# Making the weight sums of a seven-product pair ahead of the ordinary pair before it, in a two-layer hybrid block on Trainium2

## The chip, the core and the metric

The kernel runs on one core of a Trainium2 chip (trn2). The engines that matter are TensorE (PE: matmuls, with its weight loads as PEld), VectorE (DVE), ScalarE (ACT), and SyncE (SP), which issues the loads of the weights. Each engine works through its own list of instructions in the order of that list. The metric is the time of one launch in microseconds (us); lower is better.

## What is computed

Two layers on 256 tokens of width 2048, in float32: a first layer with a state-space branch and sparse attention, and a second one with compressed and selected attention and a gated delta rule. The change touches only large matrix products: one half of the first layer's output projection, both layers' feed-forward parts, two of the second layer's merge products, and its output projection. Cut to these, the reference is:

```python
x = x + concat([y_ssd, y_att]) @ w_out          # 2048 x 2048
u = rmsnorm(x, g_mlp) @ w_up                    # 2048 x 8192
x = x + square(relu(u)) @ w_down                # 8192 x 2048
...                                             # second layer: projections, attention, delta rule
x = x + (g_a * (o_a @ w_pa) + g_b * (o_b @ w_pb)) @ w_o      # g_a, g_b = sigmoid(h @ columns of w_in)
h = rms_norm(x, ln2_w)
out = rms_norm(x + square(relu(h @ w_up)) @ w_down, ln_f_w)
```

## The kernel before

Every weight is read from memory once. Weights and activations are float32 values that the kernel splits into a high and a low part, so a product of one activation block by one weight block is three matmuls: high by high, high by the weights' low part, low by high (`product`, lines 273 to 276). For a weight tile, ScalarE makes the high part (`whi`, line 281) and VectorE the low part by subtracting (`wlo`, line 282). Pools of four tiles each hold `whi` and `wlo`, so the two engines can be at most four tiles ahead of TensorE.

The function `wide` (line 251) multiplies 2048 rows of a weight by 1024 of its columns, in eight **pairs** numbered 0 to 7. A pair is two blocks of 128 rows: one transfer of 1024 KB into a tile `wst` (line 289). Three such tiles exist (`stp`, bufs=3), so the transfer of a pair can only start when the pair three places earlier has been read for the last time. A pair is one of two kinds:

- An **ordinary pair** takes eight products, 24 matmuls of 512 columns. Its weights become two `whi` and two `wlo` tiles of 1024 columns each.
- A **seven-product pair** (a step of the Strassen-Winograd scheme on 2 x 2 blocks) takes seven products, 21 matmuls. For that VectorE first makes sums of its four weight blocks: `t13` with one instruction over 1024 columns (line 303), then the two halves of `t24`, 512 columns each (lines 306 and 307). The `whi` and `wlo` tiles of the pair come in the order: two blocks of the weights themselves, `t13`, `t24`, and a last half tile of the weights.

In text below, a **four-pair call** is a call of `wide` whose pairs 1, 3, 5 and 7 are of the seven-product kind; there are twelve, six in each feed-forward part (three of `w_up`, three of `w_down`). A **three-pair call** has pairs 3, 5 and 7 of that kind; there are sixteen in the feed-forward parts beside the first call of each of them. With two first calls and five calls in the projections that makes 35 calls and 117 seven-product pairs.

Between the calls the results leave the accumulation banks, and each `w_down` call but the last ones adds its result into memory: four transfers of 512 KB each that add to what is there (line 476), issued by GpSimd. They run while the next call has begun.

The kernel's text gives each engine's instructions in program order, and when the program is built, the framework orders every engine's list anew from priorities in that order and its own idea of durations. It also adds all waits. So the list of VectorE is not the order of the text.

Of the kernel before, what the change touches and what calls it, by code (L numbers as in the profile page):

```python
# [13 lines left out]
OP = mybir.AluOpType  # L14
# [43 lines left out]
def build(ctx, tc, I, out, tap=None, upto=99):  # L58
    nc = tc.nc
    V, S, G, PE = nc.vector, nc.scalar, nc.gpsimd, nc.tensor  # L60
# [14 lines left out]
    def sp(shape, dt=F32, name="sp"):  # L75
        return sb.tile(shape, dt, name=name, tag="sp", bufs=NP)
# [13 lines left out]
    def psum(kind, shape):  # L90
        return pp.tile(shape, F32, name=kind, bufs=2)
# [159 lines left out]
    def wide(w, r0, c0, lhs, forms, order=range(8), spairs=None, hooks={}):  # L251


        ka, kb = (("mm0", "mm1"), ("tp", "sx"))[::1 - 2 * (turn[0] % 2)]
        turn[0] += 1
        B = {}

        def banks(tags, *names):
            for k, pair_ in zip(tags, names):
                for b in pair_:  # L260
                    B[b] = psum(k, [128, 512])
        banks(ka, ("P2", "P3"), ("P4", "E"))
        spairs = tuple(forms) if spairs is None else spairs
        ns = len(spairs)
        left = {b: 3 * ns + (0 if b in ("P1", "P5", "P6", "P7") else 6 * (8 - ns)) for b in ("P1", "P2", "P3", "P4", "P5", "P6", "P7", "E")}
        left["E"] = 6 * (8 - ns)
        total = dict(left)

        def mm(b, x, y):
            PE.matmul(B[b], x, y, start=left[b] == total[b], stop=left[b] == 1)  # L270
            left[b] -= 1

        def product(b, xh, xl, wa, wb):
            mm(b, xh, wa)
            mm(b, xh, wb)
            mm(b, xl, wa)

        def parts(src, n=1024):
            a = whp.tile([128, 1024], F32R, name="whi")
            b = wlp.tile([128, 1024], F32R, name="wlo")  # L280
            S.activation(a[:, :n], src, AF.Copy)  # L281
            V.tensor_tensor(b[:, :n], src, a[:, :n].bitcast(F32), op=OP.subtract)  # L282
            return [(a[:, o:o + 512], b[:, o:o + 512]) for o in range(0, n, 512)]

        for j in order:
            if j in hooks:
                hooks[j](kb)
            s = stp.tile([128, 2048], F32, name="wst")
            nc.sync.dma_start(s.rearrange("p (k n) -> p k n", k=2),
                              w[r0 + j * 256:r0 + j * 256 + 256, c0:c0 + 1024].rearrange("(k p) n -> p k n", p=128))  # L290
            if j not in spairs:
                for kk in range(2):
                    xh, xl = lhs(2 * j + kk)
                    wl = parts(s[:, kk * 1024:(kk + 1) * 1024])[::-1]
                    for i, l, b in ((0, 0, "P2"), (0, 1, "P3"), (1, 0, "P4"), (1, 1, "E")):
                        h = slice(i * 128, i * 128 + 128)
                        product(b, xh[:, h], xl[:, h], *wl[l])
                continue
            if "P1" not in B:
                banks(kb, ("P1", "P5"), ("P6", "P7"))  # L300

            t13 = sp([128, 2, 512], name="t13")
            V.tensor_tensor(t13, s.rearrange("p (k l n) -> p k l n", k=2, l=2)[:, :, 0],  # L303
                            s[:, :1024].rearrange("p (l n) -> p l n", l=2)[:, ::-1], op=OP.subtract)
            t24 = sp([128, 2, 512], name="t24")
            V.tensor_tensor(t24[:, 0], s[:, 1024:1536], t13[:, 0], op=OP.subtract)  # L306
            V.tensor_tensor(t24[:, 1], s[:, 1536:], t24[:, 0], op=OP.subtract)  # L307
            (a1h, a1l), (a2h, a2l) = lhs(2 * j), lhs(2 * j + 1)
            m1, m2 = slice(0, 128), slice(128, 256)
            sh, sl = forms[j]  # L310

            def sums(n):
                return sh[:, n - 1], sl[:, n - 1]
            w11, w22 = parts(s[:, 512:1536])
            product("P1", a1h[:, m1], a1l[:, m1], *w11)
            product("P3", *sums(4), *w22)
            u1, u3 = parts(flat(t13))
            product("P5", *sums(1), *u1)
            product("P7", *sums(3), *u3)
            u2, u4 = parts(flat(t24))  # L320
            product("P6", *sums(2), *u2)
            product("P4", a2h[:, m2], a2l[:, m2], *u4)
            (w21,) = parts(s[:, 1536:], 512)
            product("P2", a2h[:, m1], a2l[:, m1], *w21)
        return B, ka
# [67 lines left out]
    def flat(ap):  # L393
        return ap.rearrange("p k c -> p (k c)")
# [14 lines left out]
    def ffn(act, forms, xd, w_up, w_down, late, after, tail=0):  # L409
# [6 lines left out]
        for s_ in range(4):  # L416
            hT, hforms = [], {}
            for P in range(2):
                B, tags = wide(w_up, 0, s_ * 2048 + P * 1024, at_k(act), forms,
                               spairs=NPAIRS[1:] if r is None or P == 1 else NPAIRS,  # L420
                               hooks={2: hook} if r is None else {})
                us = {}
                for i, l, part, bank in shared(B, part_pairs()):
                    V.tensor_tensor(part, bank, part, op=OP.add)
                    S.activation(part, part, AF.Relu, scale=r[:, i:i + 1])
                    S.activation(part, part, AF.Square)
                    us[i, l] = part
                for l in (1, 0):
                    q = quarter("hT")
                    p = len(hT)  # L430
                    hT.append(q)
                    for k0 in range(0, 4, 2):
                        pt = psum(tags[k0 // 2], [128, 512])
                        pv = pt.rearrange("p (k t c) -> p k t c", k=2, t=2)
                        for kk in range(2):
                            for t in range(2):
                                c = (k0 + kk) * 128
                                PE.transpose(pv[:, kk, t, :], us[t, l][:, c:c + 128], ident)
                        j = 2 * p + k0 // 2
                        if j in NPAIRS:  # L440
                            f = two_forms(sp)
                            S.activation(f[0].rearrange("p k t c -> p (k t c)"), pt, AF.Copy)
                            f_to_act(f, q, k0, hforms, j)
                        else:
                            split(pt, flat(q[0][:, k0:k0 + 2]), flat(q[1][:, k0:k0 + 2]))
            for P in range(2):
# [4 lines left out]
                if (s_, P) == (3, 1):  # L451
                    for p in (2, 3):
                        ps = panel(w_down, s_ * 2048, 16, p * 512, 512, at_k(hT), tail=tail if p == 3 else 0)
                        for t in range(2):
                            V.tensor_tensor(X[p][:, t], ps[t], X[p][:, t], op=OP.add)
                            after(p, t)
                    continue
                B, _ = wide(w_down, s_ * 2048, P * 1024, at_k(hT), hforms, spairs=NPAIRS[1 - P:])
                if s_ == 3:
                    add_blocks(B, P, part_pairs())  # L460
# [396 lines left out]
    for p in range(2):  # L857
        ps = panel(I["w_out"][0], 0, 16, p * 512, 512, at_k(mix), order=list(range(8, 16)) + list(range(8)))
        for t in range(2):
            V.tensor_tensor(X[p][:, t], ps[t], X[p][:, t], op=OP.add)  # L860
        x_done(p, xn, g_mlp, ssx, xforms)
    add_blocks(wide(I["w_out"][0], 0, 1024, at_k(mix), forms_of(mix, (6, 0, 2)), (4, 5, 6, 7, 0, 1, 2, 3))[0], 1)

    def late1(tags):
# [605 lines left out]
```

## Time and profile before

| | us |
|---|---|
| median of three runs (lowest, highest) | 2688.77 (2684.59, 2689.42) |
| the profiled execution, its own time | 2686.3 |
| its span in the profile | 2684.5 |
| TensorE busy | 2612.6 (97%) |
| VectorE busy | 2138.8 (80%) |
| ScalarE busy | 1555.9 (58%) |
| granted TensorE clock, mean share of full speed | 0.996 |

The ends of matmuls in the profile are modelled and overlap, so TensorE's busy share says little on how near it is to its best pace; the starts of matmuls do. In the rows, `t` stands for `t13` and `t24`, since numbers are left out, `SPq` is SyncE's queue, and a tile's name before `<-` is what is written.

### The profile page before, as it was taken

The page shows a single profiled execution, that of the slowest core. Times are in us where ns is not written, and L with a number is a line of the kernel's source. Part 1 is how long each engine was busy: PE and PEld are TensorE (multiplying, and loading weights), DVE is VectorE, ACT ScalarE, POOL GpSimd, SP SyncE. Part 2 cuts the span into 40 slices and gives each one's busy share as a digit, 9 for nine tenths or more (in the row PEclk, how much of TensorE's full clock was granted, in tenths as well). Part 3 has the DMA queues.
Part 4 walks back from the last instruction along what each step waited for, and adds up shares of the span by engine and source line. Part 5 has one row for each costly group of instructions (what it writes and reads, how often), then busy time and mean ns, then how long its engine had stood idle before and what let it go on. Part 6 is the DMA issues. An engine that isn't in the chain of part 4 may idle for free.

```text
span 2684.5 us, 33032 instructions
## 1 busy us (share of the span) xinstructions
PE 2612.6 (97%) x12485; PEld 2153.5 (80%) x12485; DVE 2138.8 (80%) x2978; ACT 1555.9 (58%) x2098; POOL 82.6 (3%) x94
## 2 busy tenths in 40 slices
PE   8999999999999999999999999999999999999997
PEld 8988888777777777788888877888777778787776
DVE  5767789888989888676755867588999889898885
ACT  5555556666657566554533654455666566575663
POOL 0000000010000000000000000000000100000000
PEclk9999999999999999999999999999999999999999
DMA  7454555585675776653432843556655866756764
GB/s 234 152 161 162 181 194 204 188 240 199 205 235 188 220 219 204 210 193 126 137 92 81 288 136 125 175 196 214 216 204 188 231 200 205 242 188 220 219 219 141
DMA packets 191133, 512.22 MB, mean 191 GB/s; under 512 B 10151, under 2 KB 51070, under 8 KB 190974
## 3 DMA queue, kind: packets, MB, share of 16 engines
q1 hardware_dynamic: 175600, 467.57, 51.8%
q0 software_dynamic: 6912, 25.17, 5.3%
q10 hardware_dynamic: 8462, 17.37, 1.9%
q8 instruction: 98, 1.61, 0.2%
q14 instruction: 61, 0.50, 0.0%
HBM read 476.51 MB, written 33.57 MB: 190 GB/s over the span
## 4 chain that ended last, share of the span: by engine, by line
PE 63%; DVE 20%; DMA 9%; ACT 5%; issue 3%; ACTq 0%; POOL 0%; POOLq 0%; DVEq 0%; SPq 0%
PE mm L270 12%; PE mm L194 10%; PE mm L193 10%; PE mm L192 10%; DVE wlo L282 10%; PE tp L270 6%; PE sx L270 6%; DMA wst<-in_w_down_dram 4%; DMA wst<-in_w_up_dram 4%; ACT whi L281 3%; DVE t L303 2%; DVE hTl L172 1%; DVE t L307 1%; DVE t L306 1%; DVE sfl L172 1%
## 5 line engine op out<-in xcount | busy, mean ns | idle before, releaser
L282 DVE TENSOR_TENSOR wlo<-wst,whi 128x1024 fp32r<-128x1024 f32 (+1 forms) x560 | 609.2, 1109 | 83.3 <-ACT whi L281 81.5
L281 ACT ACTIVATE whi<-wst 128x1024 fp32r<-128x1024 f32 (+1 forms) x560 | 535.3, 969 | 230.1 <-PE mm L270 70.7
L208 DVE TENSOR_TENSOR wlo<-wst,whi 128x1024 fp32r<-128x1024 f32 (+6 forms) x336 | 377.2, 1128 | 209.2 <-ACT whi L207 208.3
L207 ACT ACTIVATE whi<-wst 128x1024 fp32r<-128x1024 f32 (+6 forms) x336 | 329.3, 983 | 319.6 <-PE mm L194 292.7
L281 ACT ACTIVATE whi<-t 128x1024 fp32r<-128x1024 f32 x234 | 247.7, 1059 | 322.0 <-DVE t L307 206.0
L282 DVE TENSOR_TENSOR wlo<-t,whi 128x1024 fp32r<-128x1024 f32 x234 | 284.4, 1222 | 48.0 <-ACT whi L281 44.6
L194 PE MATMUL mm<-whi,x2l 128*128 128x512 f32 (+3 forms) x608 | 229.4, 377 | 0.0
L193 PE MATMUL mm<-wlo,x2h 128*128 128x512 f32 (+3 forms) x608 | 228.1, 375 | 0.9 <-DVE wlo L208 0.8
L192 PE MATMUL mm<-whi,x2h 128*128 128x512 f32 (+3 forms) x608 | 228.0, 376 | 0.0
L303 DVE TENSOR_TENSOR t<-wst 128x1024 f32<-128x1024 f32 x117 | 142.8, 1221 | 52.5 <-DMA wst<-in_w_down_dram 27.6
L192 PE MATMUL mm<-whi,xnh 128*128 128x512 f32 (+3 forms) x416 | 152.6, 368 | 2.0 <-ACT whi L207 1.6
L193 PE MATMUL mm<-wlo,xnh 128*128 128x512 f32 (+3 forms) x416 | 151.7, 365 | 0.0
L194 PE MATMUL mm<-whi,xnl 128*128 128x512 f32 (+3 forms) x416 | 150.6, 365 | 0.1
L270 PE MATMUL mm<-wlo,xnh 128*128 128x512 f32 x377 | 148.2, 393 | 2.4 <-DVE wlo L282 2.4
L270 PE MATMUL mm<-whi,xnl 128*128 128x512 f32 x377 | 147.4, 391 | 0.0
L270 PE MATMUL mm<-whi,xnh 128*128 128x512 f32 x377 | 143.4, 393 | 0.5 <-DVE ca L336 0.5
L270 PE MATMUL mm<-wlo,hTh 128*128 128x512 f32 x328 | 129.3, 394 | 2.5 <-DVE wlo L282 2.4
L193 PEld LDWEIGHTS mm<-wlo,x2h 128*128 128x128 f32 x608 | 114.5, 188 | 16.8 <-DVE wlo L208 1.6
L270 PE MATMUL mm<-whi,hTl 128*128 128x512 f32 x328 | 127.9, 390 | 0.0
L194 PEld LDWEIGHTS mm<-whi,x2l 128*128 128x128 f32 x608 | 114.5, 188 | 15.3 <-issue 1.0
L270 PE MATMUL mm<-whi,hTh 128*128 128x512 f32 x328 | 126.2, 394 | 0.5 <-DVE ca L336 0.5
L192 PEld LDWEIGHTS mm<-whi,x2h 128*128 128x128 f32 x608 | 114.6, 189 | 15.0 <-issue 0.8
(620 smaller groups left out, 5759.4 us busy)
## 6 DMA issues: line engine op xcount, KB each, us to landing
wst<-in_w_up_dram SPq DMA_DIRECT2D x128, 1024.0 KB, 5.1
wst<-in_w_down_dram SPq DMA_DIRECT2D x128, 1024.0 KB, 5.5
wst<-in_w_in_dram SPq DMA_DIRECT2D x84, 1024.0 KB, 5.0
wst<-in_w_out_dram SPq DMA_DIRECT2D x16, 1024.0 KB, 5.8
wst<-in_w_o_dram SPq DMA_DIRECT2D x16, 1024.0 KB, 5.2
wst<-in_w_in_dram SPq DMA_DIRECT2D x16, 780.0 KB, 4.5
xd<-cd POOLq DMA_DIRECT2D x24, 512.0 KB, 10.1
wst<-in_w_in_dram SPq DMA_DIRECT2D x12, 824.0 KB, 4.6
```

Source lines behind the costliest of these rows:

```text
L172: V.tensor_tensor(lo, ps, hi.bitcast(F32), op=OP.subtract)
L192: PE.matmul(ps[t][:, :n], xh[:, sl], wa, start=kt == first, stop=False)
L193: PE.matmul(ps[t][:, :n], xh[:, sl], wb, start=False, stop=False)
L194: PE.matmul(ps[t][:, :n], xl[:, sl], wa, start=False, stop=kt == last)
L207: S.activation(a[:, :2 * n], src, AF.Copy)
L208: V.tensor_tensor(b[:, :2 * n], src, a[:, :2 * n].bitcast(F32), op=OP.subtract)
L270: PE.matmul(B[b], x, y, start=left[b] == total[b], stop=left[b] == 1)
L281: S.activation(a[:, :n], src, AF.Copy)
L282: V.tensor_tensor(b[:, :n], src, a[:, :n].bitcast(F32), op=OP.subtract)
L303: V.tensor_tensor(t13, s.rearrange("p (k l n) -> p k l n", k=2, l=2)[:, :, 0], s[:, :1024].rearrange("p (l n) -> p l n", l=2)[:, ::-1], op ...
L306: V.tensor_tensor(t24[:, 0], s[:, 1024:1536], t13[:, 0], op=OP.subtract)
L307: V.tensor_tensor(t24[:, 1], s[:, 1536:], t24[:, 0], op=OP.subtract)
```

## The change

For an ordinary pair that a seven-product pair follows, the loop now issues the transfer of the following pair and makes that pair's `t13` and `t24` before it turns to the ordinary pair's own `whi` and `wlo`. The sums are kept until the loop comes to their pair. No instruction is added or taken away. The new helper functions `load` and `sums_of` hold the lines that stood in the loop.

```diff
@@ -282,12 +282,32 @@
             V.tensor_tensor(b[:, :n], src, a[:, :n].bitcast(F32), op=OP.subtract)
             return [(a[:, o:o + 512], b[:, o:o + 512]) for o in range(0, n, 512)]
 
-        for j in order:
-            if j in hooks:
-                hooks[j](kb)
+        def load(j):
             s = stp.tile([128, 2048], F32, name="wst")
             nc.sync.dma_start(s.rearrange("p (k n) -> p k n", k=2),
                               w[r0 + j * 256:r0 + j * 256 + 256, c0:c0 + 1024].rearrange("(k p) n -> p k n", p=128))
+            return s
+
+        def sums_of(s):
+
+            t13 = sp([128, 2, 512], name="t13")
+            V.tensor_tensor(t13, s.rearrange("p (k l n) -> p k l n", k=2, l=2)[:, :, 0],
+                            s[:, :1024].rearrange("p (l n) -> p l n", l=2)[:, ::-1], op=OP.subtract)
+            t24 = sp([128, 2, 512], name="t24")
+            V.tensor_tensor(t24[:, 0], s[:, 1024:1536], t13[:, 0], op=OP.subtract)
+            V.tensor_tensor(t24[:, 1], s[:, 1536:], t24[:, 0], op=OP.subtract)
+            return t13, t24
+
+        order = list(order)
+        ready = {}
+        for n_, j in enumerate(order):
+            if j in hooks:
+                hooks[j](kb)
+            s, ts_ = ready.pop(j, (None, None))
+            s = load(j) if s is None else s
+            if j not in spairs and n_ + 1 < len(order) and order[n_ + 1] in spairs:
+                s_next = load(order[n_ + 1])
+                ready[order[n_ + 1]] = s_next, sums_of(s_next)
             if j not in spairs:
                 for kk in range(2):
                     xh, xl = lhs(2 * j + kk)
@@ -298,13 +318,7 @@
                 continue
             if "P1" not in B:
                 banks(kb, ("P1", "P5"), ("P6", "P7"))
-
-            t13 = sp([128, 2, 512], name="t13")
-            V.tensor_tensor(t13, s.rearrange("p (k l n) -> p k l n", k=2, l=2)[:, :, 0],
-                            s[:, :1024].rearrange("p (l n) -> p l n", l=2)[:, ::-1], op=OP.subtract)
-            t24 = sp([128, 2, 512], name="t24")
-            V.tensor_tensor(t24[:, 0], s[:, 1024:1536], t13[:, 0], op=OP.subtract)
-            V.tensor_tensor(t24[:, 1], s[:, 1536:], t24[:, 0], op=OP.subtract)
+            t13, t24 = sums_of(s) if ts_ is None else ts_
             (a1h, a1l), (a2h, a2l) = lhs(2 * j), lhs(2 * j + 1)
             m1, m2 = slice(0, 128), slice(128, 256)
             sh, sl = forms[j]
```

SyncE's list and GpSimd's have the same instructions in the same order as before. VectorE's list, in a four-pair call (the second half's `w_down`, `wst_7878` is pair 4 and ordinary, the seven-product pair 5 is `wst_7912` before and `wst_7880` now), from the last tile of pair 3 on. Before:

```order
L282 TENSOR_TENSOR wlo_7872<-wst_7834,whi_7871 128x512
L282 TENSOR_TENSOR wlo_7881<-wst_7878,whi_7880 128x1024
L282 TENSOR_TENSOR wlo_7897<-wst_7878,whi_7896 128x1024
L303 TENSOR_TENSOR t13_7914<-wst_7912 128x1024
L282 TENSOR_TENSOR wlo_7920<-wst_7912,whi_7919 128x1024
L306 TENSOR_TENSOR t24_7916<-wst_7912,t13_7914 128x512
L282 TENSOR_TENSOR wlo_7930<-t13_7914,whi_7929 128x1024
L307 TENSOR_TENSOR t24_7916<-wst_7912,t24_7916 128x512
L282 TENSOR_TENSOR wlo_7940<-t24_7916,whi_7939 128x1024
L282 TENSOR_TENSOR wlo_7950<-wst_7912,whi_7949 128x512
L303 TENSOR_TENSOR t13_7992<-wst_7990 128x1024
```

Now:

```order
L282 TENSOR_TENSOR wlo_7872<-wst_7802,whi_7871 128x512
L294 TENSOR_TENSOR t13_7882<-wst_7880 128x1024
L282 TENSOR_TENSOR wlo_7888<-wst_7878,whi_7887 128x1024
L297 TENSOR_TENSOR t24_7884<-wst_7880,t13_7882 128x512
L282 TENSOR_TENSOR wlo_7904<-wst_7878,whi_7903 128x1024
L298 TENSOR_TENSOR t24_7884<-wst_7880,t24_7884 128x512
L282 TENSOR_TENSOR wlo_7920<-wst_7880,whi_7919 128x1024
L282 TENSOR_TENSOR wlo_7930<-t13_7882,whi_7929 128x1024
L282 TENSOR_TENSOR wlo_7940<-t24_7884,whi_7939 128x1024
L282 TENSOR_TENSOR wlo_7950<-wst_7880,whi_7949 128x512
```

The `t13` of pair 5 stood behind both `wlo` tiles of pair 4; now it stands ahead of both, and the two halves of `t24` stand ahead of and behind the second one. Pair 3 is moved in the same way. At pair 7 `t13` stood ahead of pair 6 already, and only the halves of `t24` moved; pair 1 stays as it was.

VectorE's list in a three-pair call (`wst_7541` is the ordinary pair 4), from the last tile of pair 3 on. Before:

```order
L282 TENSOR_TENSOR wlo_7535<-wst_7493,whi_7534 128x512
L282 TENSOR_TENSOR wlo_7544<-wst_7541,whi_7543 128x1024
L282 TENSOR_TENSOR wlo_7560<-wst_7541,whi_7559 128x1024
L306 TENSOR_TENSOR t24_7579<-wst_7575,t13_7577 128x512
L282 TENSOR_TENSOR wlo_7583<-wst_7575,whi_7582 128x1024
L307 TENSOR_TENSOR t24_7579<-wst_7575,t24_7579 128x512
L282 TENSOR_TENSOR wlo_7593<-t13_7577,whi_7592 128x1024
L282 TENSOR_TENSOR wlo_7603<-t24_7579,whi_7602 128x1024
L282 TENSOR_TENSOR wlo_7613<-wst_7575,whi_7612 128x512
L303 TENSOR_TENSOR t13_7655<-wst_7653 128x1024
L282 TENSOR_TENSOR wlo_7622<-wst_7619,whi_7621 128x1024
```

Now:

```order
L282 TENSOR_TENSOR wlo_7535<-wst_7461,whi_7534 128x512
L297 TENSOR_TENSOR t24_7547<-wst_7543,t13_7545 128x512
L282 TENSOR_TENSOR wlo_7551<-wst_7541,whi_7550 128x1024
L298 TENSOR_TENSOR t24_7547<-wst_7543,t24_7547 128x512
L282 TENSOR_TENSOR wlo_7567<-wst_7541,whi_7566 128x1024
L282 TENSOR_TENSOR wlo_7583<-wst_7543,whi_7582 128x1024
L282 TENSOR_TENSOR wlo_7593<-t13_7545,whi_7592 128x1024
L282 TENSOR_TENSOR wlo_7603<-t24_7547,whi_7602 128x1024
L282 TENSOR_TENSOR wlo_7613<-wst_7543,whi_7612 128x512
L294 TENSOR_TENSOR t13_7623<-wst_7621 128x1024
L282 TENSOR_TENSOR wlo_7629<-wst_7619,whi_7628 128x1024
```

The two `t24` instructions of pair 5 moved ahead of the two `wlo` tiles of pair 4; the `t13` of pair 7 stood ahead of the tiles of pair 6 in both.

TensorE's list at the start of pair 2 (`hTh` and `hTl` are the activations) of the same four-pair call. Before:

```order
L270 MATMUL mm0_7714<-whi_7802,hTh_6980 128x512
L270 MATMUL mm0_7714<-wlo_7803,hTh_6980 128x512
L270 MATMUL mm0_7714<-whi_7802,hTl_6981 128x512
L270 MATMUL mm0_7715<-whi_7802,hTh_6980 128x512
L270 MATMUL mm0_7715<-wlo_7803,hTh_6980 128x512
L270 MATMUL mm0_7715<-whi_7802,hTl_6981 128x512
```

Now:

```order
L270 MATMUL mm0_7714<-whi_7809,hTh_6980 128x512
L270 MATMUL mm0_7715<-whi_7809,hTh_6980 128x512
L270 MATMUL mm1_7716<-whi_7809,hTh_6980 128x512
L270 MATMUL mm1_7717<-whi_7809,hTh_6980 128x512
L270 MATMUL mm0_7714<-wlo_7810,hTh_6980 128x512
L270 MATMUL mm0_7714<-whi_7809,hTl_6981 128x512
```

Four matmuls that need only `whi` now come ahead of the first that needs `wlo`. At pair 4 and pair 6 of a four-pair call TensorE's list is as before: the second matmul needs `wlo`.

## Rows read from the trace of the kernel before

**Rows 1.** The page, part 1: busy time of each engine, share of the span, instructions.

```profile
PE 2612.6 (97%) x12485; PEld 2153.5 (80%) x12485; DVE 2138.8 (80%) x2978; ACT 1555.9 (58%) x2098; POOL 82.6 (3%) x94
```

**Rows 2.** Groups by line: busy us, mean ns of one, idle before, its releasers.

```profile
L282 DVE TENSOR_TENSOR wlo<-wst,whi 128x1024 fp32r<-128x1024 f32 (+1 forms) x560 | 609.2, 1109 | 83.3 <-ACT whi L281 81.5
...
L303 DVE TENSOR_TENSOR t<-wst 128x1024 f32<-128x1024 f32 x117 | 142.8, 1221 | 52.5 <-DMA wst<-in_w_down_dram 27.6 <-DMA wst<-in_w_up_dram 23.3 <-DMA wst<-in_w_in_dram 0.8
...
L307 DVE TENSOR_TENSOR t<-wst,t 128x512 f32<-128x512 f32 x117 | 80.2, 685 | 0.1
```

**Rows 3.** Waits over the whole span: total us, times, longest us.

```profile
ACT whi L281 <- DVE t L307: 206.0, 88, 3.8
```

**Rows 4.** Timeline, VectorE, one call: start, us, line, out<-in, count [idle before <-releaser].

```profile
906.21 2.96 DVE L282 TENSOR_TENSOR wlo<-wst,whi 128x512 fp32r<-128x512 f32 x3
...
916.14 3.15 DVE L282 TENSOR_TENSOR wlo<-wst,whi 128x512 fp32r<-128x512 f32 x3
921.59 1.23 DVE L303 TENSOR_TENSOR t<-wst 128x1024 f32<-128x1024 f32 x1 [2.31 <-DMA wst<-in_w_down_dram]
...
930.38 2.35 DVE L282 TENSOR_TENSOR wlo<-wst,whi 128x1024 fp32r<-128x1024 f32 x2
```

**Rows 5.** Timeline, TensorE, the same call.

```profile
918.74 0.39 PE L270 MATMUL mm<-whi,hTh 128*128 128x512 f32 x1
918.97 0.39 PE L270 MATMUL mm<-wlo,hTh 128*128 128x512 f32 x1
...
927.52 0.50 PE L270 MATMUL sx<-whi,sfh 128*128 128x512 f32 x1 [0.36 <-ACT whi L281]
928.78 0.50 PE L270 MATMUL sx<-wlo,sfh 128*128 128x512 f32 x1 [0.76 <-DVE wlo L282]
...
931.65 0.50 PE L270 MATMUL mm<-wlo,hTh 128*128 128x512 f32 x1 [0.54 <-DVE wlo L282]
```

**Rows 6.** Timeline, SyncE, the same call: the loads of pairs 5 and 7 issued.

```profile
909.20 0.37 SPq L289 DMA_DIRECT2D wst<-in_w_down_dram  x1
...
919.31 0.37 SPq L289 DMA_DIRECT2D wst<-in_w_down_dram  x1
```

**Rows 7.** The page, part 6: a load, KB each, median us from issue to landing.

```profile
wst<-in_w_down_dram SPq DMA_DIRECT2D x128, 1024.0 KB, 5.5
```

**Rows 8.** Window, same call: us, busy by engine, granted clock, DMA share, GB/s.

```profile
913.00:921.00 8.00, 8.00 (x37) 6.61 (x36) 4.97 (x6) 3.72 (x4) 0.00 (x0) 1.00 1.03 274
```

**Rows 9.** Timeline, VectorE: the same wait in the first and the twelfth such call.

```profile
564.31 1.23 DVE L303 TENSOR_TENSOR t<-wst 128x1024 f32<-128x1024 f32 x1 [2.19 <-DMA wst<-in_w_down_dram]
...
2509.78 1.23 DVE L303 TENSOR_TENSOR t<-wst 128x1024 f32<-128x1024 f32 x1 [2.73 <-DMA wst<-in_w_up_dram]
```

**Rows 10.** Timeline, VectorE, a call with three seven-product pairs.

```profile
874.63 2.96 DVE L282 TENSOR_TENSOR wlo<-wst,whi 128x512 fp32r<-128x512 f32 x3
...
885.29 1.23 DVE L303 TENSOR_TENSOR t<-wst 128x1024 f32<-128x1024 f32 x1 [2.33 <-DMA wst<-in_w_down_dram]
886.44 2.36 DVE L282 TENSOR_TENSOR wlo<-wst,whi 128x1024 fp32r<-128x1024 f32 x2
```

**Rows 11.** Timeline, TensorE and then SyncE, that call.

```profile
887.71 0.50 PE L270 MATMUL tp<-wlo,hTh 128*128 128x512 f32 x1 [1.28 <-DVE wlo L282]
...
877.62 0.37 SPq L289 DMA_DIRECT2D wst<-in_w_down_dram  x1
```

**Rows 12.** Windows at three long TensorE waits, columns as in group 8.

```profile
1048.80:1056.00 7.20, 4.92 (x22) 3.81 (x21) 7.20 (x9) 4.56 (x5) 0.00 (x0) 1.00 0.09 14
1077.00:1081.00 4.00, 0.07 (x2) 0.03 (x1) 4.00 (x8) 1.00 (x3) 0.00 (x0) 1.00 0.69 266
1081.70:1085.10 3.40, 2.93 (x10) 2.65 (x11) 3.40 (x6) 1.96 (x5) 0.00 (x0) 0.50 0.55 219
2593.80:2596.40 2.60, 0.08 (x1) 0.00 (x0) 2.60 (x5) 1.05 (x2) 0.00 (x0) 1.00 0.23 80
2597.20:2600.60 3.40, 3.40 (x9) 2.64 (x9) 3.40 (x5) 1.14 (x2) 0.00 (x0) 0.50 0.22 48
```

## The prediction

> **What bounds the kernel now.** I read the busy times first, then the groups by line and the waits, and then one call of `wide` as a timeline. TensorE is busy 2612.6 us of the span [rows 1]. Its matmuls of 512 columns start 0.23 us apart [rows 5], so only the places where the starts are further apart can be won or lost. The change moves work on VectorE, so I ask where TensorE waits for VectorE in a call, and what VectorE waited for in turn.
>
> A four-pair call shows it. VectorE finishes the `wlo` tiles of pair 4 at 919.29 (916.14 + 3.15), then is idle for 2.31 us until the transfer of pair 5 lands, and makes its `t13` from 921.59 on [rows 4]. TensorE had begun pair 4 at 918.74 with a product of `whi`, and its first `wlo` product at 918.97 did not wait [rows 5]. It waits only later: 927.52, 928.78 (both in pair 5) and 931.65 (the first `wlo` of pair 6) are starts after a wait [rows 5]. Between 918.97 and 931.65 lie 24 + 21 = 45 matmuls, which need 10.20 us at 0.2267 us; they took 12.68. So this call loses 2.48 us there. All twelve four-pair calls have this wait of VectorE for the transfer of pair 5; the first and the last of them are in [rows 9].
>
> The transfer is late because it shares the DMA engines: from 913 to 921 they are fully busy (share 1.03, 274 GB/s) [rows 8], with the adds into memory of the call before. It was issued at 909.20, the moment that VectorE had read pair 2 for the last time (906.21 + 2.96 = 909.17) [rows 4, 6], since three `wst` tiles rotate. So the issue of a load hangs on VectorE's list, and not on where the load stands in the program.
>
> **The change part by part.** Nothing is added or removed: 117 `t13` of 1.22 us and 234 halves of `t24` of 0.685 us [rows 2] are made in either kernel.
>
> *The loads.* SyncE's list is unchanged and its loads are gated by the three tiles, so "one pair ahead" moves no issue forward. It moves some back: the last reading of pair 2 now stands behind `t13` and half of `t24` of pair 3. Successive VectorE instructions overlap by some 0.08 us, so that is about 1.14 + 0.60 = 1.74 us later. Whether the landing moves is the unknown. The DMA engines are busy anyway with the load of pair 4 and the adds [rows 8], and the load of pair 5 would stand in line behind pair 4's; so between 0 and 1.74 us. I take 0.25, near the lower end, because the window shows no free engine that an earlier issue could have used.
>
> *Pair 4 in a four-pair call (the main term).* The `wlo` tiles of pair 4 now stand behind `t13` of pair 5, which cannot start before the landing at 921.59. VectorE keeps its order, so the first `wlo` of pair 4 ends at 921.59 + 1.14 + 1.22 = 923.95 and TensorE can take it at 924.00. It wanted it at 918.97 [rows 5]: a wait of 5.03 us where there was none. In return the waits in pair 5 vanish, since all sums are done when its tiles come. Is pair 6 late? The second `wlo` of pair 4 ends at 925.7, so the load of pair 7 is issued then instead of 919.31 [rows 6]; the DMA engines have little left by then. With the median of 5.5 us for such a load [rows 7] it lands at 931.2, and pair 6's first `wlo` ends at 931.2 + 1.14 + 1.22 = 933.6. TensorE comes to it at 924.00 + 10.20 = 934.20, so it does not wait. Before, it came to it at 931.65. The call is 2.55 us longer. Both ways count from the landing, so a later or earlier landing changes the wait and not the difference, as long as both wait: 12 x 2.55 = 30.6 us. What is late next is TensorE itself, with nothing that gives the time back before the call's end.
>
> *Pair 2 in a four-pair call.* Its first `wlo` ends 1.14 us later, at 909.2 instead of 908.0 (the second of the three from 906.21 [rows 4]). TensorE began pair 2 about 45 matmuls before 918.74, at 908.54, and its new list wants that `wlo` only after four products of `whi`, at 909.45. It costs nothing, and about 0.2 us a call if the tiles come a little later.
>
> *The clock.* [...] In the stretch at 0.50 with work all through, 9 matmuls started in 3.40 us, where 15 would at full clock: 6 x 0.2267 = 1.4 us. I take 1.4 for each call: 16.8 us. Bounds: 0, if the clock holds or the slow stretch falls into the wait itself; 2.8, if it lasts twice as long.
>
> [...]
>
> *Three-pair calls.* `t13` of pair 7 stood ahead of pair 6 already, and VectorE waited for its load: 2.33 us until 885.29, and TensorE 1.28 us at 887.71 [rows 10, 11]. New is that the halves of `t24` of pair 5 stand ahead of the `wlo` tiles of pair 4, which delays the last reading of pair 4, and so the issue of pair 7's load at 877.62 [rows 11], by 2 x 0.685 = 1.37 us. The landing follows by 0 (the load stands behind that of pair 6) to 1.37 us. I take 0.6, the middle, as neither end has a nearer row: 16 x 0.6 = 9.6 us, and 0 to 22.
>
> *The other seven calls* have no adds beside them; their sums move within VectorE's idle time. Zero, with 5 us to either side.
>
> **The sum.** 30.6 + 12 x 0.25 (3.0) + 16.8 + 9.6 = 60.0 us on 2686.3, the profiled execution's own time: 2746. That execution lies 2.5 us under the median of 2688.77 and inside the runs' spread, so I do not correct for it.
>
> **The rivals.** *The waits go, and nothing takes their place (faster).* ScalarE waits 206 us in 88 places for the second half of `t24` (L307) [rows 3], and each four-pair call loses 2.48 us in pairs 5 and 6. If the sums were ready, that would be 12 x 2.48 = 29.8 us less: 2656. It decides at one point: the load of pair 5 must land 5.0 us earlier, before 916.6, so that `t13` is done when TensorE wants pair 4. Against it: the DMA engines are full until 921, and the load is issued later, not earlier. [...]
>
> *The clock holds (slower, but less).* Waits of 5 us but no stretch at 0.50: 2746 - 16.8 = 2729.
>
> *It does not do what it says (no change).* The load of pair 5 lands about 2.5 us earlier than now, so that the new wait at pair 4 just equals the old ones: 2686 and within 5 us. For it only that the adds vary from call to call: the wait was 2.19 us in the first and 2.73 in the last [rows 9].
>
> *All unknowns at their upper ends.* 30.6 + 12 x 1.74 (20.9) + 16.8 + 22 = 90 us: 2776.
>
> **How the numbers follow.** Forecast with the clock falling 0.64, the clock holding 0.16, all at the upper ends 0.07, no change 0.06, faster 0.07. The likeliest gives 2746. The range goes from 2717 (the main term alone) to 2773 and leaves out the gain, no change, and most of the worst case, together 2 in 10. A difference under 0.2% (5.4 us) can't be told from none in this kernel. Slower 0.87, same 0.06, faster 0.07.
>
> **What would show it.** Right: in the timeline of a four-pair call after, VectorE's `t13` of pair 5 still starts on the landing of its load, about 12 us after the issue, with no `wlo` of pair 4 before it; TensorE has one gap of about 5 us behind the first matmul of pair 4, twelve times; pairs 5 and 6 show none; windows right behind these gaps have a granted clock of 0.50; ScalarE's wait for L307's sums (now L298) is nearly gone. Wrong: the load of pair 5 lands less than 9 us after its issue; or the gaps stand at pair 2, where I count nothing; or the longer life of `t13` and `t24` holds back other tiles of their pool; or pair 6 waits again behind pair 4's wait, which would add up to 1 us a call.

## The result, and the profile after

The changed kernel takes 2752.18 us (median of four runs, 2746.88 to 2756.02), the kernel before 2689.1 (2684.59 to 2689.42): 1.0237 times, with a 95% interval of 1.0217 to 1.0257. The profiled execution of the changed kernel took 2752.2 us with a span of 2750.4, so 65.9 us more than the one of before in both. The forecast was 2746 with a range of 2717 to 2773.

The busy times of after, part 1 of its page (busy time, share of the span, instructions), stand beside [rows 1]: TensorE shows 23 us more with the same instructions, since matmuls take longer at half clock (records of 0.63 us against 0.39, below); VectorE's work is unchanged.

```profile
PE 2635.8 (96%) x12485; PEld 2176.7 (79%) x12485; DVE 2138.4 (78%) x2978; ACT 1560.6 (57%) x2098; POOL 79.2 (3%) x94
```

The group of `t13` (now L294), from the groups by line, answers to the L303 row of [rows 2]: VectorE's idle time ahead of it, ended by the load, has grown from 52.5 to 95.3 us. The wait of ScalarE for the second half of `t24` (L298), from the list of waits (total us, times, longest), has shrunk from 206.0 us [rows 3] to 58.3.

```profile
L294 DVE TENSOR_TENSOR t<-wst 128x1024 f32<-128x1024 f32 x117 | 142.8, 1221 | 95.3 <-DMA wst<-in_w_down_dram 45.3 <-DMA wst<-in_w_up_dram 44.8 <-DMA wst<-in_w_o_dram 3.4
```

```profile
ACT whi L281 <- DVE t L298: 58.3, 34, 3.0
```

So the change does what it says: the sums are there when they are wanted. What it costs is seen in the same `w_down` call as in [rows 4 and 5]. First the loads of pairs 5 and 7, issued by SyncE, then VectorE's timeline (start, us, line, out<-in, count, idle before and what ended it):

```profile
930.71 0.37 SPq L287 DMA_DIRECT2D wst<-in_w_down_dram  x1
...
945.58 0.37 SPq L287 DMA_DIRECT2D wst<-in_w_down_dram  x1
```

```profile
934.71 0.69 DVE L282 TENSOR_TENSOR wlo<-wst,whi 128x512 fp32r<-128x512 f32 x1
941.46 1.23 DVE L294 TENSOR_TENSOR t<-wst 128x1024 f32<-128x1024 f32 x1 [6.05 <-DMA wst<-in_w_down_dram]
942.60 1.22 DVE L282 TENSOR_TENSOR wlo<-wst,whi 128x1024 fp32r<-128x1024 f32 x1
943.73 0.68 DVE L297 TENSOR_TENSOR t<-wst,t 128x512 f32<-128x512 f32 x1
```

VectorE stands idle for 6.05 us with `t13` of pair 5 at the head of its list, waiting for a load that takes 10.75 us from issue to `t13` (930.71 to 941.46). Pair 4's first `wlo` comes behind it. TensorE, same call:

```profile
938.55 0.39 PE L270 MATMUL mm<-whi,hTh 128*128 128x512 f32 x1
943.87 0.80 PE L270 MATMUL mm<-wlo,hTh 128*128 128x512 f32 x1 [4.94 <-DVE wlo L282]
944.47 0.63 PE L270 MATMUL mm<-whi,hTl 128*128 128x512 f32 x1
944.89 0.63 PE L270 MATMUL mm<-whi,hTh 128*128 128x512 f32 x1
...
949.16 0.53 PE L270 MATMUL mm<-wlo,hTh 128*128 128x512 f32 x1
949.53 0.39 PE L270 MATMUL mm<-whi,hTl 128*128 128x512 f32 x1
949.76 0.39 PE L270 MATMUL mm<-whi,hTh 128*128 128x512 f32 x1
```

Two things are lost here. The first `wlo` matmul of pair 4 starts 5.32 us after the matmul ahead of it, so it waits 5.09. Then the matmuls start 0.43 us apart until 949.16, and 0.23 apart from 949.53 on. The windows of that call (us, busy by engine, granted clock, DMA share, GB/s) name the cause: the DMA engines full ahead of the wait (share 1.04), a clock of 0.50 for 6.8 us, from 1.3 us before the wait's end on, and 1.00 around.

```profile
933.00:938.50 5.50, 5.50 (x26) 4.56 (x25) 2.39 (x3) 2.75 (x3) 0.00 (x0) 1.00 1.04 260
938.90:942.60 3.70, 0.04 (x1) 0.00 (x0) 1.14 (x2) 1.06 (x1) 0.00 (x0) 1.00 0.99 376
942.60:949.40 6.80, 5.53 (x13) 4.37 (x14) 5.83 (x7) 1.44 (x2) 0.00 (x0) 0.50 0.42 119
949.40:956.20 6.80, 6.80 (x31) 5.61 (x31) 4.68 (x5) 3.54 (x5) 0.00 (x0) 1.00 0.36 111
```

**Where the 65.9 us are.** From the starts of the matmuls in both traces, call by call (first to last matmul of each of the 35 calls): the twelve four-pair calls take 59.6 us more, the sixteen three-pair calls of the feed-forward parts 2.1 us less, the seven other calls 5.7 us more, and 2.7 us lie between calls and in the rest of the program.

In the three-pair calls two larger changes nearly cancel. Counted by pairs, 24 or 21 matmuls in the order of TensorE's list, they lost 9.6 us at pair 6 before and lose 0.3 now; at pair 4 they lost 0.5 us and lose 7.7 now, some 0.5 us in most calls. In the call of [rows 10] that is a wait for ScalarE's `whi` (the matmul at 897.98 starts 0.62 us after the one ahead of it, 0.40 more than without a wait); what in the new order brings it is not shown.

The table takes the twelve four-pair calls apart, here and for the experiments below. "Wait at pair 4" is the start of pair 4's first `wlo` matmul less the start of the pair's first matmul, less 0.2267 us. "Behind the wait" is the time from there to pair 5's first matmul, less 23 matmuls. "Pairs 5 and 6" is the time from pair 5's first matmul to pair 7's, less 45 matmuls. All are sums over the twelve calls in us. In e1_only_pair5 the framework put two `whi` matmuls ahead of pair 4's first `wlo` matmul, not one, so there 2.7 us (12 x 0.2267) of the wait column are work and belong to the next column: 64.6 and 25.9.

| kernel | wait at pair 4 | behind the wait | pairs 5 and 6 |
|---|---|---|---|
| before | 0.1 | 0.3 | 33.2 |
| after | 66.9 | 26.4 | 0.0 |
| e1_only_pair5 | 67.3 | 23.2 | 0.0 |
| e2_all_but_pair5 | 65.8 | 24.8 | 0.0 |
| e6_all_but_pair5_kept | 0.2 | 0.3 | 38.0 |
| e4_before_no_adds | 0.0 | 0.0 | 2.8 |
| e5_after_no_adds | 0.0 | 0.1 | 0.0 |
| e3_fill | 70.2 | 1.6 | 0.2 |
| e8_sums_behind | 0.1 | 0.2 | 24.2 |
| e10_t24_first | 0.0 | 0.1 | 14.0 |

### The profile page after: what moved, and what is told of

The parts are those of the page before. It is cut to its first block, busy times and chain, and to the rows that moved or that the text cites. A ratio compares the mean times of both kernels' runs of the same rounds, so it can differ in the third digit from the quotient of the medians.

```text
span 2750.4 us, 33036 instructions
## 1 busy us (share of the span) xinstructions
PE 2635.8 (96%) x12485; PEld 2176.7 (79%) x12485; DVE 2138.4 (78%) x2978; ACT 1560.6 (57%) x2098; POOL 79.2 (3%) x94
## 3 DMA queue, kind: packets, MB, share of 16 engines
q0 software_dynamic: 6912, 25.17, 5.2%
## 4 chain that ended last, share of the span: by engine, by line
PE 71%; DVE 15%; DMA 6%; ACT 5%; issue 2%; POOL 0%; ACTq 0%; DVEq 0%; POOLq 0%; SPq 0%
PE mm L270 17%; PE mm L194 10%; PE mm L193 10%; PE mm L192 10%; PE tp L270 9%; PE sx L270 8%; DVE wlo L282 6%; ACT whi L281 3%; DMA wst<-in_w_down_dram 3%; DMA wst<-in_w_up_dram 3%; DVE t L294 2%; DVE hTl L172 1%; DVE t L297 1%; PE sx L1062 1%; DVE t L298 1%
## 5 line engine op out<-in xcount | busy, mean ns | idle before, releaser
L282 DVE TENSOR_TENSOR wlo<-wst,whi 128x1024 fp32r<-128x1024 f32 (+1 forms) x560 | 617.8, 1109 | 122.7 <-ACT whi L281 121.4
L294 DVE TENSOR_TENSOR t<-wst 128x1024 f32<-128x1024 f32 x117 | 142.8, 1221 | 95.3 <-DMA wst<-in_w_down_dram 45.3
```

## Experiments: which of the moved sums costs

**Only pair 5.** The condition of the change, narrowed to pair 5 of the four-pair calls:

```diff
-            if j not in spairs and n_ + 1 < len(order) and order[n_ + 1] in spairs:
+            if j == 4 and len(spairs) == 4:
```

> The kernel before, with only pair 5 of the twelve four-pair calls treated as in the change: its sums stand ahead of pair 4's own tiles. Theory (t13 of pair 5 waits at the head of VectorE's list for a late load and holds back pair 4's wlo; the wait then costs half clock): the whole loss is here, 12 x 5 us, so 2745 to 2751. Rival (the loss is spread over all the sums that the change moves, as a delay of VectorE's other work): twelve of some ninety moved pairs, so about +8 us, 2697.

Measured: 2740.58 us, 1.0203 times before (1.0186 to 1.0220). A little under the stated 2745, but 54 of the change's 63 us are in these twelve sums of the 117. VectorE and then TensorE in the same call:

```profile
942.13 1.22 DVE L294 TENSOR_TENSOR t<-wst 128x1024 f32<-128x1024 f32 x1 [4.69 <-DMA wst<-in_w_down_dram]
943.27 1.22 DVE L282 TENSOR_TENSOR wlo<-wst,whi 128x1024 fp32r<-128x1024 f32 x1
```

```profile
944.54 0.79 PE L270 MATMUL mm<-wlo,hTh 128*128 128x512 f32 x1 [4.57 <-DVE wlo L282]
945.13 0.63 PE L270 MATMUL mm<-whi,hTl 128*128 128x512 f32 x1
```

**All but pair 5, in the text.** The same condition, with pair 5 left out:

```diff
-            if j not in spairs and n_ + 1 < len(order) and order[n_ + 1] in spairs:
+            if j not in spairs and n_ + 1 < len(order) and order[n_ + 1] in spairs and not (j == 4 and len(spairs) == 4):
```

> The changed kernel, but pair 5 of the twelve four-pair calls keeps its sums at the old place. Theory: the sixteen three-pair calls and the seven other calls together cost little, 0 to +9 us over the kernel before, 2689 to 2698; pair 7 of the four-pair calls may add up to 0.5 us each. Rival (loss spread over all moved sums): +50 us or more, 2739.

Measured: 2745.58 us, 1.0226 times before (1.0209 to 1.0242): the theory's number is missed by 48 us, and the rival's is met. But the kernel is not what the edit meant. VectorE's timeline:

```profile
941.00 1.22 DVE L294 TENSOR_TENSOR t<-wst 128x1024 f32<-128x1024 f32 x1 [5.93 <-DMA wst<-in_w_down_dram]
942.14 2.35 DVE L282 TENSOR_TENSOR wlo<-wst,whi 128x1024 fp32r<-128x1024 f32 x2
944.41 0.68 DVE L297 TENSOR_TENSOR t<-wst,t 128x512 f32<-128x512 f32 x1
```

The framework, which orders the lists anew, put `t13` of pair 5 ahead of pair 4's two `wlo` tiles although the text had it behind them; only the halves of `t24` went back. So this run tells something else: `t13` alone in that place is enough for nearly the whole loss (65.8 and 24.8 us in the table).

**All but pair 5, in the list.** In addition to the condition of the last run, an order-only dependency holds `t13` where the kernel before had it (`first` is the instruction of `t13`, `last[0]` that of the latest `wlo`; the second value of `n_` keeps pair 7's place as in the changed kernel):

```diff
+            if len(spairs) == 4 and n_ in (5, 6) and last[0] is not None:
+                tc.add_manual_dep(first.ins if hasattr(first, 'ins') else first, (last[0].ins if hasattr(last[0], 'ins') else last[0]).name, mybir.DependencyInfo(mybir.DependencyClass.NoSync, mybir.DependencyReason.DATA), reason="order")
```

> The changed kernel, but in the twelve four-pair calls the t13 of pair 5 is held by an order-only dependency behind both wlo tiles of pair 4, as in the kernel before; pairs 1, 3 and 7 and all other calls are as in the changed kernel. Theory (t13 of pair 5 ahead of pair 4's tiles is what costs): no wait at pair 4 and no stretch at half clock; what is left is the rest of the change, about +1.2 us in each of the two first calls and some us elsewhere, and the old losses in pairs 5 and 6: 2685 to 2700. Rival (any sums moved ahead cost as much): 2735 or more.

Measured: 2692.67 us, 1.0026 times before (1.0016 to 1.0036), as the theory has it, and 53 us under the last run, from which it differs only by the dependency. VectorE and TensorE in the same call are back at the rows of before ([rows 4 and 5]), with waits in pairs 5 and 6 and none at pair 4:

```profile
915.67 2.59 DVE L284 TENSOR_TENSOR wlo<-wst,whi 128x1024 fp32r<-128x1024 f32 x2 [1.03 <-ACT whi L283]
920.69 1.23 DVE L296 TENSOR_TENSOR t<-wst 128x1024 f32<-128x1024 f32 x1 [2.43 <-DMA wst<-in_w_down_dram]
```

```profile
926.62 0.50 PE L270 MATMUL sx<-whi,sfh 128*128 128x512 f32 x1 [0.33 <-ACT whi L283]
927.88 0.50 PE L270 MATMUL sx<-wlo,sfh 128*128 128x512 f32 x1 [0.76 <-DVE wlo L284]
930.75 0.49 PE L270 MATMUL mm<-wlo,hTh 128*128 128x512 f32 x1 [0.52 <-DVE wlo L284]
```

The other moved sums together cost about 8 us (6.9 between the two traces). Of these, 4.7 are in the four-pair calls, all of it in pair 5, where `t13` starts 0.42 us later on average than before; 3.3 are in the seven other calls, 2.3 of them in the first two of the program (the output projection and the first `w_up` call, +1.15 and +1.14). The three-pair calls take 5.4 us less, and 4.3 us more lie between calls; no run takes these apart.

## Experiments: why `t13` waits, and what the wait costs beside itself

**Without the adds.** From each of the two kernels the transfers that add the `w_down` results into memory are taken out. They are 48 in all, four in each of twelve `w_down` calls; the 24 of the two expectations are those of one block (`cd`) alone:

```diff
-                for src in (pairs, banks):
-                    for l in range(2):
-                        G.dma_start(xd[:, 2 * P + 1 - l], src[l], accum_op=OP.add)
```

> The kernel before without the 24 transfers that add the w_down results into memory (these results are left out of x). Theory (the adds make the load of pair 5 late): t13 of pair 5 no longer waits for its load, the 2.5 us that each four-pair call loses in pairs 5 and 6 shrink by more than half, so 15 to 35 us less than the kernel before: 2651 to 2671. Rival (the load is late for another reason): within 5 us of 2686.

> The changed kernel without the 24 transfers that add the w_down results into memory (these results are left out of x). Theory: with the load of pair 5 landed in time, the sums ahead of pair 4 wait for nothing, the twelve waits of 5 us and the half clock are gone, and the kernel comes to within 10 us of the kernel before without the adds, 2651 to 2680. Rival (VectorE's order alone, without the late load, holds back pair 4): the difference between the two stays near 60 us.

Measured: 2656.18 us for the kernel before without adds (0.9886, 0.9868 to 0.9904) and 2653.31 for the changed one (0.9875, 0.9857 to 0.9893). Both are in the theory's ranges: the difference of 63 us is gone, and the sign has turned by 3 us. VectorE still waits up to 0.85 us for the load of pair 5, but well ahead of TensorE's need. VectorE and SyncE in the changed kernel without adds, same call:

```profile
903.46 0.69 DVE L282 TENSOR_TENSOR wlo<-wst,whi 128x512 fp32r<-128x512 f32 x1
904.96 1.23 DVE L294 TENSOR_TENSOR t<-wst 128x1024 f32<-128x1024 f32 x1 [0.81 <-DMA wst<-in_w_down_dram]
906.10 1.22 DVE L282 TENSOR_TENSOR wlo<-wst,whi 128x1024 fp32r<-128x1024 f32 x1
```

```profile
899.46 0.37 SPq L287 DMA_DIRECT2D wst<-in_w_down_dram  x1
```

The load is issued 7.83 us before TensorE's pair 4 on average, as in the changed kernel with the adds, but in this call it is there 5.50 us after its issue, against 10.75, and `t13` starts 2.3 us before TensorE's pair 4, not 2.9 us after it. In these calls the order of VectorE's list is the same in both; what differs is the landing. So the list makes the wait possible, and the adds in the DMA engines make it happen.

**The clock by itself.** Behind the first matmul of pair 4, 22 matmuls by a block of zeros keep TensorE busy through the wait:

```diff
+        def product(b, xh, xl, wa, wb, fill=0):
             mm(b, xh, wa)
+            for _ in range(fill):
+                PE.matmul(B[b], zero, wa, start=False, stop=False)
             mm(b, xh, wb)
...
+                        product(b, xh[:, h], xl[:, h], *wl[l], fill=22 if j == 4 and len(spairs) == 4 and kk == 0 and b == "P2" else 0)
```

The kernel also holds the `t13` of pair 7 behind the last tile of pair 5 with the order-only dependency shown above, and VectorE's list is then that of the changed kernel, but for the one instruction that makes the zeros.

> The changed kernel, with 22 matmuls by a block of zeros behind the first matmul of pair 4 in the twelve four-pair calls; they add zero to the result and fill 22 x 0.227 = 5.0 us of TensorE's wait. VectorE's list is as in the changed kernel. Theory (the half clock after the wait costs about 2.75 us a call, by itself): the wait for wlo stays where it was, the clock holds at 1.00, and the time falls by 12 x 2.75 = 33 us to about 2719. Rival (after the wait the landing and VectorE set the pace, not the clock): the same time as the changed kernel, 2752, give or take 5.

Measured: 2727.26 us, 1.0155 times before (1.0136 to 1.0175); 25 us less than the changed kernel, where 33 were expected and the rival had none. TensorE's timeline, and windows from the pair's start on:

```profile
934.49 0.40 PE L272 MATMUL mm<-whi,hTh 128*128 128x512 f32 x1
934.72 5.30 PE L278 MATMUL mm<-whi,zero 128*128 128x512 f32 x22
940.00 0.50 PE L272 MATMUL mm<-wlo,hTh 128*128 128x512 f32 x1
940.34 0.39 PE L272 MATMUL mm<-whi,hTl 128*128 128x512 f32 x1
```

```profile
934.50:939.80 5.30, 5.30 (x24) 4.12 (x22) 2.21 (x2) 1.93 (x2) 0.00 (x0) 1.00 0.84 313
939.80:946.60 6.80, 6.80 (x30) 5.47 (x30) 6.22 (x8) 1.89 (x3) 0.00 (x0) 1.00 0.47 152
```

`wlo` comes as late as before the fill, and the clock now holds at 1.00. In the table, the time behind the wait falls from 26.4 to 1.6 us; the waits were 3.3 us longer in this trace (later landings), so the twelve calls gain 21.5 us. The two traces differ by 26.9 us; 3.4 of the rest are in one `w_o` call (the section on the prediction comes to it). The clock's price is real and by itself: 24.8 / 12 = 2.1 us a call, not the 2.75 that I had read from one call.

## Experiments: the opposite order

**Sums behind the ordinary pair.** The kernel before, with the dependency shown above under another condition: pair 7's `t13` behind pair 6's tiles, where the list of before had it ahead.

```diff
+            if j == 7 and last[0] is not None:
...
```

> The kernel before with the change reversed at pair 7: its t13 is made to stand behind the wlo tiles of the ordinary pair 6, where before it stood ahead of them in the four-pair and the three-pair calls. Theory (sums that wait for a load ahead of an ordinary pair's tiles are what costs): pair 6 no longer waits, 0.5 us in each four-pair call and 1.3 us in each three-pair call, so up to 27 us less, 2662 to 2680. Rival (the wait comes back in pair 7, whose sums are then late): no change, 2689 give or take 5.

Measured: 2674.82 us, 0.9957 times before (0.9942 to 0.9972): faster, and inside the theory's range. VectorE in a three-pair call, where TensorE has no wait at pair 6 any more (1.28 us in [rows 11] for the call of that kind shown there, 1.37 in this one):

```profile
704.00 2.54 DVE L284 TENSOR_TENSOR wlo<-wst,whi 128x1024 fp32r<-128x1024 f32 x2 [1.00 <-ACT whi L283]
706.45 1.22 DVE L305 TENSOR_TENSOR t<-wst 128x1024 f32<-128x1024 f32 x1
```

The wait of `t13` for its load (2.11 us in this call before) is gone too: the load has landed by 706.45, when VectorE is done with pair 6's tiles. Of the up to 27 us, 11.5 came. Not every three-pair call had such a wait to lose (the `w_up` call ahead of the one of [rows 10] had none), and in the four-pair calls 9.0 us are won in pairs 5 and 6 (33.2 to 24.2) but 4 come back earlier in the calls. Pair by pair, TensorE's loss at pair 6 goes from 10.1 to 0.0 us in the twelve four-pair calls and from 9.6 to 0.0 in the sixteen three-pair calls, so the theory's wait is gone everywhere; it was worth 19.7 us, not 27. Against that, the first pair of the calls (pair 0) loses 4.1 and 2.7 us more, and pair 5 of the four-pair calls 1.2; why pair 0 does is open.

What is left in pair 5 of the four-pair calls shows in VectorE's list there: behind the second half of `t24` it waits for ScalarE's `whi` of `t24`.

```profile
920.41 0.68 DVE L311 TENSOR_TENSOR t<-wst,t 128x512 f32<-128x512 f32 x1
922.30 1.23 DVE L284 TENSOR_TENSOR wlo<-t,whi 128x1024 fp32r<-128x1024 f32 x1 [1.21 <-ACT whi L283]
```

**Both halves of `t24` first.** On top of it, in pair 5, the `wlo` tile of `t13` behind both halves of `t24` (`both` is the second half's instruction, `behind` the same order-only dependency):

```diff
             u1, u3 = parts(flat(t13))
+            if j == 5:
+                behind(last[0], both)
```

> The kernel with pair 7's sums behind pair 6's tiles, and in addition both halves of t24 of pair 5 ahead of the wlo tile of t13, in place of between the tiles. Theory (pair 5's loss hangs on the chain landing, t13, t24, ScalarE's whi of t24, its wlo): the chain is one wlo, 1.14 us, shorter, so some 0.9 us of the 2.0 us that the twelve calls still lose in pair 5 go: 11 us under that kernel, about 2664. Rival (the sum of VectorE's work after the landing sets it, whatever its order): the same time as that kernel, 2675.

Measured: 2663.35 us, 0.9911 times before (0.9891 to 0.9930), as the theory has it. VectorE and then TensorE in the `w_down` call:

```profile
911.86 1.23 DVE L308 TENSOR_TENSOR t<-wst 128x1024 f32<-128x1024 f32 x1 [2.22 <-DMA wst<-in_w_down_dram]
913.00 1.22 DVE L287 TENSOR_TENSOR wlo<-wst,whi 128x1024 fp32r<-128x1024 f32 x1
914.14 0.69 DVE L313 TENSOR_TENSOR t<-wst,t 128x512 f32<-128x512 f32 x1
914.86 0.69 DVE L314 TENSOR_TENSOR t<-wst,t 128x512 f32<-128x512 f32 x1
915.47 2.52 DVE L287 TENSOR_TENSOR wlo<-t,whi 128x1024 fp32r<-128x1024 f32 x2
```

```profile
916.74 0.50 PE L270 MATMUL tp<-wlo,sfh 128*128 128x512 f32 x1 [0.45 <-DVE wlo L287]
```

VectorE makes the tiles of `t13` and `t24` in one stretch of 2.52 us, without the 1.21 us of waiting for ScalarE between them, and one wait of 0.45 us is left in pair 5. The loss of pairs 5 and 6 is 14.0 us for twelve calls. This kernel is about 89 us faster than the changed one, and beats the kernel before by 21.

A fourth `wst` tile, with which the load itself could start earlier, was not tried.

## Why the prediction was right

The sign, the mechanism and the time (2752 in 2717 to 2773) are right. That the sum is only 6 us off is in part luck: three terms were off, and the clock (9.6 us too low) and the three-pair calls (11.7 us too high) nearly cancel; most of what is left is the other calls (8.4 us too low).

| term | forecast, us | in the traces, us |
|---|---|---|
| new wait at pair 4, less the old losses, with the later landing | 30.6 + 3.0 | 66.9 - 33.2 - 0.4 = 33.3 |
| half clock behind it | 16.8 | 26.4 |
| sixteen three-pair calls | 9.6 | -2.1 |
| seven other calls and the rest | 0 | 5.7 + 2.7 |
| sum | 60.0 | 66.0 |

- **The main term** was right in its parts: a wait of 5.09 us in the call that was worked out (forecast 5.03), and no wait left in pairs 5 and 6. Over the twelve calls the wait was 5.6 us on average and the old loss 2.8, both some 0.3 us more than in that call, so their difference holds. That it hangs on pair 5's `t13` and on nothing else in the change is shown by e1 and e6, that `t13` alone is enough by e2 beside e6, and that it hangs on the late load by e5.
- **The landing.** The load was issued later, as forecast: 1.71 us in each of the twelve calls, counted from pair 4's first matmul (1.74 forecast). The start of `t13`, counted in the same way, went from 3.01 us to 3.39 on average (36.1 and 40.7 us in sum). So 0.38 us a call, where 0.25 was taken. How much of that is the later issue is not shown: in e1 the load is issued as early as before, and `t13` starts at 3.42. At most a small part of the 1.71 us reaches the landing, as the reading of [rows 8] had it.
- **The clock** was mis-sized: 1.4 us a call, measured 2.2 (26.4 / 12). That the clock falls was right: it was 0.50 behind all twelve waits of 4.95 to 6.09 us, and with the waits filled (e3) 1.6 us were left of the 26.4. The step that failed was to take the length of the stretch at 0.50 from [rows 12], 3.4 us behind waits of 4.0 and 2.6 us, with work all through it. In eleven of the twelve calls it lasted 6.8 us. The cost of each is here half of what is left of it when the wait ends: in the call above it ends at 949.4 and the wait at 943.87, so 5.5 / 2 = 2.8 (measured 2.73); in the second four-pair call it was granted from 614.9 on and the wait ended at 618.35, so 3.4 / 2 = 1.7 (1.71). This gives each of the twelve within 0.1 us. The part that fell into the wait cost nothing. So both cases of the forecast's bounds came together, a stretch twice as long and a part of it within the wait; the twelve costs lie between 1.6 and 2.7 us.
- **Three-pair calls** were the wrong sign: 9.6 us forecast, 2.1 us less measured. The step that failed was "the landing follows by 0 to 1.37 us": over the sixteen calls `t13` of pair 7 starts 2.68 us before TensorE's pair 6 on average, where it started 1.93 before, and the loss at pair 6 is gone (9.6 to 0.3 us). And the forecast had no term for pair 4, where 7.2 us more are lost than before. Pair 7's load in the call of [rows 10 and 11] was issued later, as forecast, but took 5.49 us to `t13` (899.67 to 905.16, below), not 7.67 (877.62 to 885.29): it now stands 3.47 us behind the load of pair 6 in SyncE's queue (896.20), where it stood 2.27 behind (875.35). That the two loads got into each other's way less is likely by this, but no run shows it. VectorE waits 0.74 us for it, not 2.33.

```profile
899.67 0.37 SPq L287 DMA_DIRECT2D wst<-in_w_down_dram  x1
```

```profile
905.16 1.23 DVE L294 TENSOR_TENSOR t<-wst 128x1024 f32<-128x1024 f32 x1 [0.74 <-DMA wst<-in_w_down_dram]
```

- **The other calls** were put at zero, with 5 us either side, and cost 5.7, with 2.7 beside. 1.2 each are in the output projection and the first `w_up` call, in every kernel that moves their sums and not in e1. 3.8 are in one `w_o` call of this execution (1.9 in the execution of e2, 1.8 in that of e6, 0.4 in that of e3). The step that failed is "their sums move within VectorE's idle time". In that `w_o` call the `t13` of pair 6 now stands ahead of the ordinary pair 5's `wlo` and waits for its load, and TensorE waits with it (2.12 us, last section): the main term's mechanism once more, in a call without adds beside it.

```profile
1922.25 1.23 DVE L294 TENSOR_TENSOR t<-wst 128x1024 f32<-128x1024 f32 x1 [3.01 <-DMA wst<-in_w_o_dram]
```

The same matmul waits 1.64 us in e2 and 1.43 in e6, and not at all in e1, where these sums are not moved, nor in e3; what decides how late that load lands, and what makes the 2.7 us between calls, stays open.

- **The rivals.** The faster one was decided at "the load of pair 5 must land 5.0 us earlier". Without the adds `t13` of the changed kernel starts 2.7 us ahead of pair 4 on average, 5.7 us earlier than in the kernel before, and the changed kernel is then the faster one: the point was right, and the adds are what keeps it from being reached. The price of that rival was not right: it is faster by 3 us, not 30, since the earlier landing alone takes the loss in pairs 5 and 6 from 33.2 to 2.8 us in the order of before (e4). To place the sums sooner wins these 3 us without the adds, and loses 63 with them because the sums' own input does not come sooner. The clock did not hold (0.50 behind each of the twelve waits).

## What to carry to other kernels

On an engine that works through its list in order, as VectorE did here, moving work ahead of other work helps only if its input is already there: otherwise its wait becomes the wait of all that stands behind it (6.05 us at `t13`, and 5.09 for TensorE, in the call above). So ask of a moved instruction when its last input lands in the worst place, here beside the adds (10.75 us from issue to use), and put what is ready first; moving the sums the other way, behind the ordinary pair's tiles, gained 0.4%, and shortening the chain behind the landing another 0.5%. And read the list as built, since the order of the text is not the order of the engine.

## What the hardware showed that was not expected

- The stretch at half clock after a wait of about 5 us was 6.8 us long in eleven of twelve calls and 3.4 in the twelfth. That wait was the shortest (4.95 us), but the length of the wait does not decide it: in e2 two waits of 5.17 and 5.47 us had 3.4 us behind them and one of 4.86 had 6.8. What does stays open; in the twelfth call the clock fell only 0.4 us after the wait had ended. Its window:

```profile
2574.20:2577.60 3.40, 3.40 (x10) 2.63 (x9) 3.40 (x5) 0.00 (x0) 0.00 (x0) 0.50 0.33 70
```

- A much shorter wait cost the clock too. In the `w_o` call named above a matmul waited 2.12 us, ending at 1924.66, and 1.0 us later the clock was at 0.50 for 3.4 us; a wait of some 2.3 us in [rows 12] had left it at 1.00.

```profile
1924.66 0.50 PE L270 MATMUL mm<-wlo,mTh 128*128 128x512 f32 x1 [2.12 <-DVE wlo L282]
```

```profile
1925.70:1929.10 3.40, 3.40 (x9) 2.63 (x8) 3.40 (x4) 0.11 (x1) 0.00 (x0) 0.50 0.38 104
```

- A load of 1024 KB beside the adds took 10.75 us from issue to use, and 5.50 without them, although the adds of a call are only 2048 KB. In the trace of before, the transfers of 913 to 921 us by queue (packets, MB, share of the DMA engines' time) show how so few bytes weigh: the adds (q0, whose 25.17 MB over the whole span are the 48 adds of 512 KB) took 64.3% for 1.00 MB, the loads (q1) 38.8% for 1.19 MB, so an add took about twice a load's time for each byte here.

```profile
q0 software_dynamic: 274, 1.00, 64.3%
q1 hardware_dynamic: 309, 1.19, 38.8%
```
